# Ordering the down projection of a hybrid decoder block as one list of steps

## The chip, the cores and the metric

The kernel runs on one core of a Trainium2 chip. The metric is the device time of one execution in microseconds (us), lower is better. Three executions of the kernel before are shown; one further execution was profiled.

## What is computed

The reference is one decoder block on 512 tokens of width 2048, in float32. Only its last sub-layer is touched by the change; the rest is named so that the stages can be placed.

```python
mod = silu(c) @ w_ada + b_ada                    # six rows: shift, scale, gate, twice
h = rmsnorm(x, g1) * (1 + sc1) + sh1
mix = concat(rwkv7(h @ w_in), pool(h @ w_in)) @ w_out
x = x + gt1 * mix
h = rmsnorm(x, g2) * (1 + sc2) + sh2
u = h @ w_up                                     # 2048 -> 2 x 5632
val, gate = split(causal_conv3(u) + conv_b)
x = x + gt2 * ((silu(gate) * val) @ w_down)      # 5632 -> 2048: the down projection
out = rmsnorm(x, g_final)
```

## The kernel before

**Precision.** Every float32 product is made of three matmuls (`mm3`, L133): weight and activation are each split into a high part (a cast on ACT) and a low part (a subtraction on DVE), and PE computes high x high (L135), high x low (L136) and low x high (L137). A block of up to eight weight tiles of 128x128 (a 128x1024 row) is split by `wsplit` (L1381): the cast is L1387, the subtraction L1388. The result goes into one of three buffers, `w0`, `w1` and `w2`, in turn, so a cast cannot start before PE has finished with the block three back.

**The down projection** begins after the last pair of the up projection (about 1670 us of 2161). Its 44 activation tiles `ad[j]` lie in device memory. There are 16 output rows of 128 features, and four parts:

- *Plain* (`plain`, L1675): tiles 0 to 7, each of the 16 rows, eight weight tiles with 512 columns: 24 matmuls a row. The result is copied to `yd[f]` in device memory (`stored`, L1697). Between the rows, `operands` prepares the operands of the next part; two of them (T3 and T4) are held back and made later by `last_operands` (L1579).
- *Strassen group* (`strassen`, L1711): tiles 8 to 23, in a 2x2 scheme with seven products per pair of rows instead of eight. For each f from 0 to 7 the order is Y11, (T4 of the f before, in `last_down`, L1703), Y21, T1, T2, Y22, T3; each is 24 matmuls of 256 columns. The weights of T1, T2, Y22 and T3 are sums on DVE over 128x1024 quarters (r1 L1736, r2 L1743, r4 L1750, r3 L1757); r2 needs r1 and r4 needs r2. Partial results are read out by ACT (L1725, L1738, L1745, L1707) and DVE (L1731, L1752, L1759), and added into `yd` by POOL's DMA queue (L1753, L1708).
- *Rest in full width*: tiles 24 to 43 (20 tiles, in blocks of 8, 8 and 4), output rows 0 to 7 with 512 columns. The activations are loaded in place and split (`act_pair_inplace`, L1508: cast L1515, subtraction L1516). The first four rows go through `down_four` (L1816) block by block; the others one after the other.
- *Rest in halves*: the output rows 8 to 15, first for columns 0 to 255, then for 256 to 511 (`down_half`, L1850), in steps of 24, 24 and 12 matmuls.

**Around it.** Each output row needs an element of the last gate `gt2`: `gate_row` (L1807) multiplies a 128x2048 row of `w_ada` with silu(c) on DVE (L1812) and adds the bias (L1813); `gate_load` (L1802) fetches the row two ahead on SP's queue. `load_x2` (L1841) fetches the residual and the `yd` sum and joins them on DVE (L1845). `last_residual` (L1857) adds the row (DVE L1264), squares it (ACT L1255 or L1251), sums the squares (DVE L1256) and scales it (ACT L1859).

**What sets the order.** In this part nothing but the dependences and a priority by the place in the program: a scheduler of the compiler picks each engine's next instruction. Two places say more: the three matmuls of a block that is held back are threaded singly between those of the next block by `tc.issue_after` (in `mm3`), and `gate_row` is queued behind the last weight subtraction in the same way. Other parts of the kernel (L452, L1157) are under `tc.manual_schedule()`, where each engine takes its instructions in the order in which the program emits them. Either way the program of an engine is one fixed list; what differs is who chose its order.

**Buffers.** Weight rows of the plain part and of the rest land in three buffers of `wide` (in the rest two halves of `wd2` besides); the sums r1 to r4 use the same three. The quarters of the Strassen group use two pairs of buffers (`wd4`).

Of the kernel before, what the change touches and what calls it, by code (L numbers as in the profile page):

```python
# [16 lines left out]
P = 128  # L17
# [10 lines left out]
NSLOT = 10  # L28
NB = 10
# [38 lines left out]
def block_kernel(ctx, tc, a, out, stop=None, dbg=None):  # L68
# [64 lines left out]
    def mm3(ps, wh, wl, xh, xl, start, stop, more=False, hold=False):  # L133
# [1374 lines left out]
    def act_pair_inplace(i, u, g, eng):  # L1508
# [70 lines left out]
    def last_operands(name):  # L1579
        for h in held:  # L1580
            if h[0] != name:
                continue
            if len(h) == 4:
                make(name, h[1], pairwise(h[2]), 2, h[3])
                h[2].done()
            else:
                make(*h)
# [87 lines left out]
    def plain(acts, k0):  # L1675

        nk = len(acts)
        for f in range(KT):
            w = wide("wd").rearrange("p a b -> p (a b)")
            nc.sync.dma_start(w, a["wdn"][f, :, k0 * P : (k0 + nk) * P])  # L1680
            wh, wl = wsplit(w, 0)
            ps = bank()
            for k in range(nk):
                sl = slice(k * P, (k + 1) * P)
                mm3(ps, wh[:, sl], wl[:, sl], acts[k][:, 0, :], acts[k][:, 1, :], start=k == 0, stop=k == nk - 1,
                    hold=f == KT - 1 and k == nk - 1)
            if f == 0:
                last_product(pend)
            if f < KT - 1:
                stored(f, ps)  # L1690
            for _ in range(2 if f else 1):
                next(prep, None)
        for _ in prep:
            pass
        return lambda: stored(KT - 1, ps)
# [7 lines left out]
    def last_down(p):  # L1703

        f, u2, b, w22 = p
        product(b, w22, ops["T4"], start=False)
        S.activation(u2[:, H0], b, AF.Copy, scale=-1.0)  # L1707
        G.dma_start(yd[f], u2.t, accum_op=ALU.add)  # L1708
        u2.done()

    def strassen(hook):  # L1711

        wq = [rb.tile([P, 4 * QW], F32, tag=f"x2_{i}", name="wd4") for i in (0, 2, 1, 3)]
        pend = None
        for f in range(NWF):
            wa, wb = wq[2 * (f % 2)], wq[2 * (f % 2) + 1]
            w11, w12, w21, w22 = (t[:, s_] for t in (wa, wb) for s_ in (W1, W2))
            nc.sync.dma_start(wa, a["wdn"][f, :, ND * P : 3 * ND * P])
            nc.sync.dma_start(wb, a["wdn"][f + NWF, :, ND * P : 3 * ND * P])
            pa = bank()[:, 0:HT]  # L1720
            cap = Slot("cap")
            product(pa, w11, ops["Y11"])
            if f == 0:
                finish_plain()
            S.copy(cap[:, H0], pa)  # L1725
            if pend:
                last_down(pend)
            u1 = Slot("u1")
            pb = bank()[:, 0:HT]
            product(pb, w12, ops["Y21"])  # L1730
            V.tensor_add(u1[:, H0], cap[:, H0], pb)  # L1731
            hook(f, 0)
            u2 = Slot("u2")
            pc = bank()[:, 0:HT]
            r1 = wide("r1").rearrange("p a b -> p (a b)")
            V.tensor_add(r1, w21, w22)  # L1736
            product(pc, r1, ops["T1"])
            S.copy(cap[:, H1], pc)  # L1738
            if f == 0:
                last_operands("T3")  # L1740
            hook(f, 1)
            r2 = wide("r2").rearrange("p a b -> p (a b)")
            V.tensor_add(r2, r1, w11)  # L1743
            product(pa, r2, ops["T2"], start=False)
            S.copy(cap[:, H0], pa)  # L1745
            if f == 0:
                last_operands("T4")
            hook(f, 2)
            r4 = wide("r4").rearrange("p a b -> p (a b)")
            V.tensor_add(r4, r2, w12)  # L1750
            product(pc, r4, ops["Y22"], start=False)
            V.tensor_add(u1[:, H1], cap[:, H0], pc)  # L1752
            G.dma_start(yd[f], u1.t, accum_op=ALU.add)  # L1753
            u1.done()
            hook(f, 3)
            r3 = wide("r3").rearrange("p a b -> p (a b)")
            V.tensor_add(r3, w11, w21)  # L1757
            product(pa, r3, ops["T3"], start=False)
            V.scalar_tensor_tensor(u2[:, H1], pa, -1.0, cap[:, H1], op0=ALU.mult, op1=ALU.subtract)  # L1759
            cap.done()  # L1760
            pend = (f + NWF, u2, pa, w22)
        return pend

    def rest_pair(eng):
# [228 lines left out]
```

## Time and profile before

| What | Value |
|---|---|
| median of three runs | 2163.02 us (2159.95 to 2188.56) |
| the profiled execution | 2162.7 us, its span 2160.9 us |
| mean granted TensorE clock | 0.992 |
| PE busy | 2110.9 us, 98% |
| DVE busy | 1678.0 us, 78% |
| ACT busy | 1047.8 us, 48% |
| POOL busy | 237.0 us, 11% |

| Stretch of the trace, us | what runs | PE busy | DVE busy | ACT busy | DMA share |
|---|---|---|---|---|---|
| 1700 to 1750 | plain | 50.00 | 19.56 | 16.78 | 0.47 |
| 1800 to 1850 | Strassen group | 50.00 | 38.28 | 22.66 | 0.55 |
| 1900 to 1950 | its last f, start of the rest | 46.36 | 31.88 | 22.01 | 1.00 |
| 1950 to 2000 | rest, full width | 47.63 | 40.99 | 18.20 | 0.86 |
| 2050 to 2100 | rest, halves | 50.00 | 31.24 | 29.64 | 0.63 |

How to read it. The span is the traced part of an execution; the time of the run is 1.8 us longer. Engine rows give a start, a duration, the engine, the line of the kernel and the tile names, output first; in square brackets stands how long the engine sat idle before and who released it. The ends of matmuls are modelled and matmuls overlap, so their starts are to be compared, not their durations.

### The profile page before, as it was taken

Reading aid. Unit: us, or ns where it says so; the run is one execution under the profiler, and the core shown is the slowest. Engines: PE = TensorE matmul, PEld = TensorE weight load, DVE = VectorE, ACT = ScalarE, POOL = GpSimd, SP = SyncE. Lnnn points to the kernel's source line nnn. Section 1 sums busy time; section 2 is a strip of 40 time slices with the busy share of each in tenths; the row PEclk is TensorE's granted clock in tenths of the full one; section 3 lists DMA queues with packets and bytes.
Section 4 is the critical chain, followed back from the end, with each engine's and each line's share of the span. In section 5 each row is a group of like instructions: output and inputs, shape, how many; then the busy total and the mean of one; then the engine's idle time right before and its main releaser. Section 6 shows DMA issues by size and latency. Waiting matters only on the chain.

```text
span 2160.9 us, 44013 instructions
## 1 busy us (share of the span) xinstructions
PE 2110.9 (98%) x17864; PEld 1866.0 (86%) x17864; DVE 1678.0 (78%) x2615; ACT 1047.8 (48%) x1510; POOL 237.0 (11%) x376
## 2 busy tenths in 40 slices
PE   7999999999999999999999999999999999999997
PEld 3567777777767888999999999999999889987897
DVE  7998898988853678888888887777788657768764
ACT  4354444433433466555555555555556444443353
POOL 0002122221100101110110000000000000120000
PEclk9999999999999999999999999999999999999998
DMA  9976676656537565989888877777777635598764
GB/s 395 393 229 197 200 199 174 199 170 186 150 105 263 183 197 176 290 241 260 253 241 255 236 209 205 207 208 210 209 209 219 211 118 144 161 318 311 243 195 167
DMA packets 169485, 471.89 MB, mean 218 GB/s; under 512 B 21361, under 2 KB 29505, under 8 KB 159169
## 3 DMA queue, kind: packets, MB, share of 16 engines
q1 hardware_dynamic: 120370, 352.12, 48.1%
q0 software_dynamic: 27696, 79.20, 17.5%
q10 hardware_dynamic: 21216, 37.76, 5.7%
q8 instruction: 140, 2.29, 0.4%
q14 instruction: 63, 0.52, 0.1%
HBM read 432.81 MB, written 36.18 MB: 217 GB/s over the span
## 4 chain that ended last, share of the span: by engine, by line
PE 86%; DMA 5%; DVE 4%; ACT 2%; issue 2%; POOL 1%; POOLq 0%; ACTq 0%; DVEq 0%; SPq 0%
PE b L137 19%; PE b L135 19%; PE b L136 19%; PE mm L645 11%; PE pf L426 4%; PE b L1217 2%; PE b L1218 1%; DMA wrow<-wup 1%; PE pb L1047 1%; DVE war L764 1%; DMA wraw<-wout 1%; DMA wa<-ada 1%; PE pa L711 0%; ACT x L1317 0%; DMA wraw<-win 0%
## 5 line engine op out<-in xcount | busy, mean ns | idle before, releaser
L137 PE MATMUL b<-t,uw 128*128 128x256 f32 x1408 | 388.6, 276 | 0.0
L135 PE MATMUL b<-t,uw 128*128 128x256 f32 x1408 | 388.6, 276 | 0.0
L136 PE MATMUL b<-t,uw 128*128 128x256 f32 x1408 | 388.6, 276 | 0.0
L135 PE MATMUL b<-y,uw 128*128 128x256 f32 x1056 | 293.6, 278 | 4.1 <-ACT uw L1387 4.1
L137 PE MATMUL b<-y,uw 128*128 128x256 f32 x1056 | 292.8, 278 | 0.8 <-DVE uw L1388 0.7
L136 PE MATMUL b<-y,uw 128*128 128x256 f32 x1056 | 292.9, 277 | 0.0
L645 PE MATMUL mm<-ahl,whi 128*128 128x512 f32 x864 | 289.7, 409 | 2.1 <-DVE rk L548 1.4
L135 PEld LDWEIGHTS b<-t,uw 128*128 128x128 f32 x1408 | 264.3, 188 | 0.0
L136 PEld LDWEIGHTS b<-t,uw 128*128 128x128 f32 x1408 | 264.3, 188 | 0.0
L137 PEld LDWEIGHTS b<-t,uw 128*128 128x128 f32 x1408 | 264.3, 188 | 0.0
L1388 DVE TENSOR_TENSOR uw<-r,uw 128x1024 fp32r<-128x1024 f32 x164 | 200.6, 1224 | 76.7 <-ACT uw L1387 76.7
L1388 DVE TENSOR_TENSOR uw<-wquart,uw 128x1024 fp32r<-128x1024 f32 x156 | 190.9, 1224 | 68.0 <-ACT uw L1387 67.0
L1387 ACT CAST uw<-wquart 128x1024 fp32r<-128x1024 f32 x156 | 164.1, 1052 | 88.9 <-PE b L137 66.0
L135 PEld LDWEIGHTS b<-y,uw 128*128 128x128 f32 x1056 | 199.5, 189 | 4.8 <-ACT uw L1387 4.8
L137 PE MATMUL b<-act,uw 128*128 128x256 f32 (+1 forms) x608 | 200.5, 330 | 2.7 <-DVE uw L1388 2.7
L1388 DVE TENSOR_TENSOR uw<-wd,uw 128x1024 fp32r<-128x1024 f32 (+1 forms) x112 | 124.1, 1109 | 101.1 <-ACT uw L1387 100.3
L1387 ACT CAST uw<-r 128x1024 fp32r<-128x1024 f32 x164 | 172.5, 1052 | 60.6 <-PE b L137 60.6
L135 PE MATMUL b<-act,uw 128*128 128x256 f32 (+1 forms) x608 | 200.7, 330 | 0.0
L137 PEld LDWEIGHTS b<-y,uw 128*128 128x128 f32 x1056 | 199.5, 189 | 1.2 <-DVE uw L1388 1.2
L136 PE MATMUL b<-act,uw 128*128 128x256 f32 (+1 forms) x608 | 200.4, 330 | 0.0
L136 PEld LDWEIGHTS b<-y,uw 128*128 128x128 f32 x1056 | 199.6, 189 | 0.1
L645 PEld LDWEIGHTS mm<-ahl,whi 128*128 128x128 f32 x864 | 158.2, 188 | 43.2 <-issue 12.2
(356 smaller groups left out, 4601.2 us busy)
## 6 DMA issues: line engine op xcount, KB each, us to landing
wquart<-wup SPq DMA_DIRECT2D x176, 512.0 KB, 5.2
wa<-ada SPq DMA_DIRECT2D x48, 1024.0 KB, 9.1
war<-ada SPq DMA_DIRECT2D x192, 256.0 KB, 3.8
wd<-wdn SPq DMA_DIRECT2D x64, 512.0 KB, 4.1
wraw<-win ACTq DMA_DIRECT2D x118, 256.0 KB, 4.1
wraw<-wout SPq DMA_DIRECT2D x96, 256.0 KB, 3.5
wquart<-wup POOLq DMA_DIRECT2D x44, 512.0 KB, 6.8
r<-wup SPq DMA_DIRECT2D x44, 512.0 KB, 4.7
```

What stands on the lines that cost most here:

```text
L135: muls = [lambda: PE.matmul(ps, wh, xh, start=start, stop=False, skip_group_check=more), lambda: PE.matmul(ps, wh, xl, start=False, stop=F ...
L136: lambda: PE.matmul(ps, wh, xl, start=False, stop=False, skip_group_check=more),
L137: lambda: PE.matmul(ps, wl, xh, start=False, stop=stop, skip_group_check=more)]
L426: PE.matmul(pf[n % 2 * 4 + ii], w[:, sl], full[k], start=k == 0, stop=k == KT - 1)
L645: PE.matmul(ps, w[:, sl], x, start=first, stop=k == KT - 1 and i == 2)
L764: V.scalar_tensor_tensor(wa, wa, 1.0, cqs[kq], op0=ALU.mult, op1=ALU.mult, accum_out=modq[:, kq, j : j + 1])
L1047: PE.matmul(pt[HS[e], h, c * 2 * L : (c + 1) * 2 * L], nt[HS[e], s, :], rw[HS[e], s, :, :], start=True, stop=True)
L1217: PE.matmul(ps[:, :].rearrange("p (a b) -> p a b", a=2), wh, x, start=start, stop=False)
L1218: PE.matmul(ps[:, 0:HT], wl, x[:, 0, :], start=False, stop=stop)
L1387: S.copy(hi, src)
L1388: lo_of[0] = V.tensor_tensor(lo, src, hi.bitcast(F32), op=ALU.subtract)
```

## The change

The whole down projection, with the last product of the up projection as its second entry, becomes a list of `Step` objects. A step has an optional load, a block to split (perhaps after a sum on DVE), its matmuls, and a list of things to do after. `pipeline` emits them: at step i its matmuls, then the load of step i+4, then the sum and split of step i+2, then what follows step i. The matmuls that are held back move their "after" list to the next step. All of this stands under `tc.manual_schedule()`, so each engine and each DMA queue follows this order. `issue_after` goes away in both places.

Other moves: the activations of the rest are loaded (`rest_load`) and split (`rest_split`) at separate steps; T3 is made after the last plain row, T4 after the first two products of the group; loading the residual and joining it are separate (`fetch_x2`, `join_x2`), and the fetches of rows 0 to 3 come in the second block round of the rest, no longer during the group; the gate rows hang on fixed steps. The set of products, sums, splits and transfers is unchanged.

```diff
+LA = 4
...
             for m in (late.pop(0), muls[1], late.pop(0), muls[2], late.pop(0)):
-                with tc.issue_after(ins.ins):
-                    ins = m()
+                ins = m()
...
+    def rest_load(i, eng):
+        u, g = REST[i]
         pool, tag = UNITS[u][g]
         t = pool.tile([P, 2, 2, T], F32R, tag=tag, name="act2")
         for n in range(2):
-            raw = t[:, 1, n, :].bitcast(F32)
-            eng.dma_start(raw, ad[2 * i + n])
-            S.copy(t[:, 0, n, :], raw)
-            V.tensor_tensor(t[:, 1, n, :], raw, t[:, 0, n, :].bitcast(F32), op=ALU.subtract)
-        return [t[:, :, n, :] for n in range(2)]
+            eng.dma_start(t[:, 1, n, :].bitcast(F32), ad[3 * ND + 2 * i + n])
+        A3.extend([t[:, :, n, :] for n in range(2)])
+
+    def rest_split(i):
+        for t in A3[2 * i : 2 * i + 2]:
+            S.copy(t[:, 0, :], t[:, 1, :].bitcast(F32))
+            V.tensor_tensor(t[:, 1, :], t[:, 1, :].bitcast(F32), t[:, 0, :].bitcast(F32), op=ALU.subtract)
...
+    def pipeline(steps):
...
+        def split(st):
+            st.w = wsplit(st.raw(), st.off)
+
+        for i in range(LA):
+            ahead(i, load)
+        ahead(0, split)
+        ahead(1, split)
+        carried = []
+        for i, st in enumerate(steps):
+            st.mm(*st.w)
+            ahead(i + LA, load)
+            ahead(i + 2, split)
+            todo, carried = carried + ([] if st.hold else st.after), st.after if st.hold else []
+            for fn in todo:
+                fn()
...
+    def plain_steps():
...
+            after = [lambda f=f, ps=ps: stored(f, ps[0]), lambda f=f: spread(2 if f > 1 else 1)]
+            if f == KT // 2 + 2:
+                after.append(lambda: pair_load(0))
...
+        out_[-1].after += [lambda: last_operand("T3", 0), lambda: last_operand("T3", 1)]
...
+    def group_steps():
...
+            def total(d, name, x, y):
+                d[name] = wide(name).rearrange("p a b -> p (a b)")
+                V.tensor_add(d[name], x(), y())
+                return d[name]
...
+            out_.append(Step(w11, mul(d, "a", "Y11"), [p1], off=16))
+            if before:
+                out_.append(before)
+            out_ += [Step(w12, mul(d, "b", "Y21"), [p2], off=16),
+                     Step(lambda d=d, x=w21, y=w22: total(d, "r1", x, y), mul(d, "c", "T1"), [p3], off=16),
+                     Step(lambda d=d, y=w11: total(d, "r2", lambda: d["r1"], y), mul(d, "a", "T2", False), [p4], off=16),
+                     Step(lambda d=d, y=w12: total(d, "r4", lambda: d["r2"], y), mul(d, "c", "Y22", False), [p5], off=16),
+                     Step(lambda x=w11, y=w21: total({}, "r3", x, y), mul(d, "a", "T3", False), [p6], off=16)]
+            before = Step(w22, mul(d, "a", "T4", False), [p7], off=16)
             if f == 0:
...
+                out_[0].after.append(lambda: last_operand("T4", 0))
+                out_[1].after += [lambda: last_operand("T4", 1), lambda: pair_load(1)]
+            elif f + 1 < NWF:
+                out_[-5].after.append(lambda f=f: pair_load(f + 1))
+        p = out_[-7:]
+        p[0].after += [lambda: rest_load(0, G), lambda: rest_load(1, G)]
+        p[2].after += [lambda: rest_load(2, G), lambda: rest_load(3, G)]
+        for i in range(4):
+            p[3 + i].after.append(lambda i=i: rest_split(i))
...
     def gate_row():
         i = gated[0]
         gated[0] += 1
-        with tc.issue_after(lo_of[0].ins):
-            m = mod[:, 80 + i : 81 + i]
-            V.scalar_tensor_tensor(wa2[i], wa2[i], 1.0, cb[0], op0=ALU.mult, op1=ALU.mult, accum_out=m)
-            V.tensor_add(m, m, cols("b_ada", 80 + i, 81 + i))
+        m = mod[:, 80 + i : 81 + i]
+        V.scalar_tensor_tensor(wa2[i], wa2[i], 1.0, cb[0], op0=ALU.mult, op1=ALU.mult, accum_out=m)
+        V.tensor_add(m, m, cols("b_ada", 80 + i, 81 + i))
         gate_load(i + 2)
...
+    for b, (k0, n) in enumerate(BLOCKS):
+        for f in range(4):
...
+            if b == 1:
+                st.after.append(lambda f=f: fetch_x2(f))
+            if b == 2:
+                st.after.append(lambda f=f: join_x2(f))
+            if 2 * b + f > 1 and f % 2:
+                st.after.append(gate_row)
+            if b == 2:
+                st.after.append(lambda f=f: residual_of(f, four[f][1]))
+    for f in range(4, NWF):
+        sts, ps = rest_steps(f)
+        sts[0].after += [lambda f=f: fetch_x2(f), gate_row]
+        sts[1].after.append(gate_row)
+        sts[2].after += [lambda f=f: join_x2(f), lambda f=f, ps=ps: residual_of(f, ps)]
+        steps += sts
+    for hf in range(2):
+        for f in range(NWF, KT):
+            sts, ps = rest_steps(f, hf)
+            n = f - NWF
+            if hf == 0:
+                sts[0].after.append(lambda f=f: fetch_x2(f))
+                if n in (0, 2, 4):
+                    sts[1].after.append(gate_row)
+                sts[2].after.append(lambda f=f: join_x2(f))
+            sts[2].after.append(lambda f=f, ps=ps, hf=hf: residual_of(f, ps, hf))
...
+    with tc.manual_schedule():
+        pipeline(steps)
```

More of the change, by code (lines that the diff above doesn't have):

```diff
@@ L1673, in block_kernel, with __init__ @@
     yd = [tc.dram_tile([P, T], F32, name=f"yd{f}") for f in range(KT)]
[L1675 to L1695, printed above, removed]
+    class Step:
+        def __init__(self, raw, mm, after=(), load=None, off=0, hold=False):
+            self.raw, self.mm, self.after, self.load, self.off, self.hold = raw, mm, list(after), load, off, hold
@@ new lines, in pipeline, with ahead, load @@
+    def pipeline(steps):
+        def ahead(i, what):
+            if i < len(steps):
+                what(steps[i])
+        def load(st):
+            if st.load:
+                st.load()
+        def split(st):
[12 more added lines that the diff above has]
+                fn()
@@ L1701, in stored @@
         s_.done()
[L1703 to L1714, printed above, removed]
-        for f in range(NWF):
[L1716 to L1722, printed above, removed]
-            if f == 0:
[L1724 to L1762, printed above, removed]
```

232 lines of the change are left out of this document (145 added, 87 removed).

## The prediction

> **What bounds the kernel now.** I read the whole page first, then the windows of the down projection, then PE's waits in it, then the timeline of single engines around each wait. The page's first line, and four windows in which PE has gaps beside one in which it has none (PE, PEld, DVE, ACT, POOL busy; granted clock; DMA share; GB/s):
>
> ```profile
> span 2160.9 us, 44013 instructions
> ```
> ```profile
> 1900.00:1910.00 10.00, 8.24 (x73) 8.05 (x72) 6.75 (x9) 4.43 (x7) 5.58 (x10) 1.00 0.87 263
> 1910.00:1920.00 10.00, 8.12 (x57) 7.92 (x56) 6.03 (x8) 6.34 (x11) 0.00 (x0) 0.83 1.03 394
> 1970.00:1980.00 10.00, 7.79 (x35) 6.12 (x33) 10.00 (x14) 7.85 (x11) 1.10 (x2) 1.00 0.87 309
> 1980.00:1990.00 10.00, 9.84 (x43) 8.18 (x44) 10.00 (x14) 1.30 (x2) 0.78 (x2) 1.00 0.94 334
> 1800.00:1810.00 10.00, 10.00 (x90) 10.00 (x90) 7.25 (x8) 4.75 (x6) 0.86 (x1) 1.00 0.62 184
> ```
>
> PE is the bound. Its waits from 1660 us to the end, those of the closing norm left out (waiter, releaser: total, times, longest):
>
> ```profile
> PE b L137 <- DVE uw L1388: 4.5, 3, 2.4
> PE b L135 <- ACT cap L1738: 1.9, 1, 1.9
> ```
>
> PE stands still for 4.5 + 1.9 = 6.4 us. The timeline of PE shows the two stops of the last Strassen f, and what follows them:
>
> ```profile
> 1906.01 0.28 PE L136 MATMUL b<-T,uw 128*128 128x256 f32 x1
> 1908.04 0.38 PE L137 MATMUL b<-T,uw 128*128 128x256 f32 x1 [1.75 <-DVE uw L1388]
> ...
> 1910.55 0.28 PE L137 MATMUL b<-T,uw 128*128 128x256 f32 x1
> 1912.70 0.38 PE L135 MATMUL b<-Y,uw 128*128 128x256 f32 x1 [1.88 <-ACT cap L1738]
> ...
> 1914.37 0.42 PE L136 MATMUL b<-Y,uw 128*128 128x256 f32 x1
> ...
> 1917.57 0.31 PE L136 MATMUL b<-T,uw 128*128 128x256 f32 x1
> ```
>
> From 1914.37 to 1917.57 there are 15 starts, 0.213 us apart; at full speed 24 matmuls of this size take 2.72 us (next fence), 0.113 apart. So these two stops were followed by 3.2 us at half rate, in the window with the granted clock of 0.83; cost 15 x 0.10 = 1.5, with its edges 1.6 us. All that an order of work can win here is 6.4 + 1.6 = 8.0 us, 0.37% of the span. The longest stop, 2.4 us, lies at the end of the window from 1970, where DVE is busy for 10.00 of 10 us.
>
> **The change part by part.** It adds and removes no matmul, cast, sum or byte. What it moves is the order on ACT, DVE, POOL and SP. So each term is a lateness: when the split of step i+2 ends against the moment when PE wants it. The rows of a regular period of the group:
>
> ```profile
> 1800.02 1.05 ACT L1387 CAST uw<-wd 128x1024 fp32r<-128x1024 f32 x1 [1.67 <-PE b L137]
> ...
> 1819.06 1.05 ACT L1387 CAST uw<-wd 128x1024 fp32r<-128x1024 f32 x1 [1.67 <-PE b L137]
> ```
> ```profile
> 1801.10 1.23 DVE L1388 TENSOR_TENSOR uw<-wd,uw 128x1024 fp32r<-128x1024 f32 x1 [0.66 <-ACT uw L1387]
> 1804.09 1.23 DVE L1388 TENSOR_TENSOR uw<-r,uw 128x1024 fp32r<-128x1024 f32 x1 [1.77 <-ACT uw L1387]
> 1805.35 1.22 DVE L1757 TENSOR_TENSOR r<-wd,wd 128x1024 f32<-128x1024 f32 x1
> ...
> 1808.07 1.23 DVE L1736 TENSOR_TENSOR r<-wd 128x1024 f32<-128x1024 f32 x1
> 1809.22 0.41 DVE L1731 TENSOR_TENSOR u<-cap,b 128x256 f32<-128x256 f32 x1
> 1809.55 1.22 DVE L1388 TENSOR_TENSOR uw<-r,uw 128x1024 fp32r<-128x1024 f32 x1
> ```
>
> Seven steps take 1819.06 - 1800.02 = 19.04 us, 2.72 a step. Cast to subtraction is 1.08. A 1024-wide DVE operation delays the next by 1.14 (1808.07 to 1809.22) when that stands ready, and by 1.26 (1804.09 to 1805.35) behind one that waited; the 256-wide one by 0.33. In this order r3, and r1 of the next f, are summed well ahead of the casts that read them, between other work. In the list each sum stands directly ahead of its own split on DVE: sum, cast, subtraction, next sum, with no overlap.
>
> *Group, f from 1 to 6.* Zero is the end of T3's matmuls. The cast of w12 starts at 0, its subtraction at 1.08, sum r1 at 2.22, cast 3.47 (sum 1.22 plus 0.03), subtraction 4.55; r2: sum 5.69, subtraction 8.02; u1's addition 9.16; r4: sum 9.49, subtraction 11.82; r3: sum 12.96, subtraction 15.29 to 16.52. PE wants it at 6 x 2.72 = 16.32: 0.2 late. With 1.26 in place of 1.14 it is 0.65. After r3 three steps without sums restore the phase. I take 0.2 x 6 = 1.2 us (long: 0.65 x 6 = 3.9).
>
> *Group, f = 0.* The list puts T3, held over from the last plain row, and half of T4 between r1 and r2, and the rest of T4 between r2 and r4. In the trace r1 of f = 0 was summed in the plain stage, under cover, and the held operands went through back to back, two 512-wide in 1.29, 0.6 each:
>
> ```profile
> 1740.26 1.23 DVE L1736 TENSOR_TENSOR r<-wd 128x1024 f32<-128x1024 f32 x1
> ...
> 1761.90 1.29 DVE L1529 TENSOR_TENSOR T<-t,T 128x512 fp32r<-128x512 f32 x2
> ```
>
> Zero is the start of Y11. PE: Y11 with three held 512-wide matmuls (twice the columns, 0.23 each) ends at 3.4, Y21 at 6.12, T1 at 8.84. The cast of r1 waits for the buffer that the held matmuls read: 1.2; subtraction 2.28; DVE then does T3 (two 512-wide and one 1024-wide, which waits for its cast) and half of T4 until 7.12; sum r2 7.12, subtraction 9.45 to 10.68, wanted at 8.84: 1.85 late. T2 ends at 13.4; T4's second half and sum r4 (12.06) bring r4's subtraction to 15.6: 2.2 late; r3 follows 0.8 late. Sum 4.9 (long: 6.0). Nothing hides it: PE's next block waits.
>
> *Last f.* The four splits of rest activations come after T1, T2, Y22 and T3, each two 512-wide casts and subtractions (1.2 on DVE). Two lie between r4's subtraction and the sum r3: r3's subtraction ends at 17.7 against 16.32, 1.4 late (long 2.7). The stops of 1.75 and 1.88, behind casts that waited for these loads, and the half rate go away: the loads are now ahead of the residual's on POOL.
>
> *Third block round of the rest.* Four steps of 12 matmuls, 2.72 us each, carry four joins, four residuals and two gate rows. The rows for it:
>
> ```profile
> 1956.82 2.28 DVE L1812 SCALAR_TENSOR_TENSOR wa<-wa,cb 128x2048 f32<-128x2048 f32 x1
> ...
> 1959.34 0.75 DVE L1845 SCALAR_TENSOR_TENSOR x<-yd,mod,x 128x512 f32<-128x512 f32 x1
> ...
> 1969.21 0.75 DVE L1264 SCALAR_TENSOR_TENSOR x<-b,mod,x 128x512 f32<-128x512 f32 x1 [1.37 <-PE b L137]
> ```
> ```profile
> 1969.21 0.63 ACT L1387 CAST uw<-wd 128x512 fp32r<-128x512 f32 x1 [2.10 <-PE b L137]
> 1970.00 0.64 ACT L1251 ACTIVATE acc<-x 128x512 f32<-128x512 f32 x1 [0.16 <-DVE x L1264]
> 1970.67 0.82 ACT L1859 ACTIVATE x<-x,eps,vec 128x512 f32<-128x512 f32 x1
> ```
>
> A gate row takes 2.5 (1956.82 to 1959.34). Zero is the start of row 0's block. Residual 0 at 2.72, square 3.5, scaling 4.17, cast of row 3's block 4.9, subtraction 5.55; join 1 6.15; gate row 6.85; residual 1 9.35; square 10.1; scaling 10.8; only then ACT casts the first block of row 4, 11.5 to 12.6, subtraction 12.6 to 13.85. PE wants it at 4 x 2.72 = 10.88: 3.0 late. Behind the gate row of row 3 (19.5 to 22.0) two further blocks are 0.8 and 0.9 late. Sum 4.7 (long 5.8), in place of the stop of 2.4.
>
> *Halves.* Three gate rows hang on the middle step of rows 8, 10 and 12, a row being 2.72 + 2.72 + 1.36 = 6.8 us. DVE needs 1.14 + 1.14 + 0.6 for splits, 0.75 + 0.4 + 0.33 for join, residual and sum, and 2.5: 6.9. The cast of the 12-matmul block stands behind square and scaling, which wait for the residual, which waits for the gate row: some 0.75 late at rows 10 and 12, 1.8 at row 8, where the held row's residual comes on top. Sum 3.3 (long 6.0).
>
> *Elsewhere nothing.* A plain row gives 5.44 us for one split and two operand pieces (1.14 + 2 x 1.14 on DVE); loads four ahead have three buffers, which the split two ahead frees in time. The last column half has no gate row and no join. Taking `issue_after` away leaves PE's order as it was.
>
> *The half rate.* It came after two stops of 1.75 and 1.88 some 4.7 us apart, and not after the single 2.4. At f = 0 stand 1.85 and 2.2 next to one another: I take it once, 1.6 (between 0 and 3.2). [...]
>
> **The sum.** 4.9 + 1.2 + 1.4 + 4.7 + 3.3 + 1.6 = 17.1, less the 8.0 of now: +9.1 us. With the long spacings 6.0 + 3.9 + 2.7 + 5.8 + 6.0 + 3.2 = 27.6, +19.6; short and with no half rate, +7.5. The profiled execution took 2162.7 us (span 2160.9 and 1.8 around it), 0.3 below the median of 2163.02. I forecast 2162.7 + 9.1 = 2171.8 us. I take the short spacings because most of the operations in these places stand ready behind one another.
>
> **The rivals.**
>
> *Not slower.* One mechanism: DVE's lateness stays inside the two steps of lead. It decides at f = 0: if r2's subtraction ends before 8.84, neither it nor r4 stops PE, and if the cast for row 4 is out before 10.88, the third round does not either. Then 8.0 goes and 1.2 + 1.4 comes: 2162.7 - 8.0 + 2.6 = 2157.3 us. For it speaks that the stops of now are all of work set far ahead, in front of near work; against it, that DVE was already full at 1970 to 1980.
>
> *The change does not do what it says.* If the compiler's choice was near the list already, or the list binds only part of the engines, the stops stay where they are: 2160 to 2166 us. Against it speak the sums, made up to half a period earlier now than the list has them.
>
> *Row loads stuck on SP.* `gate_load` waits on SP for its gate row, and the row loads stand behind it. The page's issue group, and the landing times of the row loads (shortest, median, longest):
>
> ```profile
> wa<-ada SPq DMA_DIRECT2D x48, 1024.0 KB, 9.1
> ```
> ```profile
> DMA to landing us min/median/max: 2.6/4.5/13.2
> ```
>
> In the third round the load behind the gate row that ends at 22.0 lands at 26.5 by the median and at 35.2 by the longest; its split, 2.3 us, is wanted at 34.6. So 2.9 us late at worst, and only then; at each of nine gate rows it makes 26 us on top: 2198 us. For it speaks a DMA share of 0.87 and over; against it the median.
>
> **How the numbers follow.** Forecast 0.60 (its own range 2166 to 2182), not slower 0.20, no effect 0.12, stuck loads 0.08. The range reaches to the other cases on both sides: 2157 to 2184 us; below lies half of the second case, above most of the last. Faster by over 2% (43 us, about what a measurement of this kernel can tell from no change) would need five times what is there: 0.01. Slower by over 2%: 0.03, from stuck loads worse than worked out. Within 2%: 0.96.
>
> **What would show it.** Right: in the group, DVE going sum, cast, subtraction without overlap, and a PE stop of some 0.2 to 0.65 us ahead of T3 in each f; stops of about 2 us ahead of T2 and Y22 of f = 0; one of about 3 us ahead of row 4's first block, released by L1388; no stop behind the loads of rest activations. Wrong: PE without stops at f = 0, or ACT waiting for row loads by DMA. The forecast as a whole is wrong if the time is below that of before.

## The result and the profile after

| | before | after |
|---|---|---|
| median of 22 executions each, in turn | 2161.24 us | 2175.58 us |
| median of the 18 shorter executions of each | 2161.19 us | 2174.61 us |
| profiled execution | 2162.7 us | 2173.78 us |
| ratio to before, 95% interval | | 1.0072 (1.0046 to 1.0098) |

Some executions of most kernels here take about 30 us longer than the others; from the second row of the table on the medians leave these out, while the ratios and their intervals still hold a few of them. The change costs 0.72% by the ratio, some 15.6 us, and 13.4 us by the medians of the second row; forecast were 9.1. The page's first line for the kernel after:

```profile
span 2171.9 us, 44015 instructions
```

PE's waits from 1660 us to the end in the kernel after (waiter, releaser: total, times, longest), the closing norm's left out:

```profile
PE b L138 <- DVE uw L1388: 5.8, 13, 0.8
PE b L136 <- ACT uw L1387: 3.4, 3, 1.6
...
PE b L136 <- ACT cap L1812: 1.2, 1, 1.2
```

Before there were 6.4 us in four waits; now there are 10.4 in 17, none longer than 1.6. They stand almost all ahead of a block that has just been split (L1387, L1388). The windows of the kernel after, with the same columns as in the prediction, show where:

```profile
1770.00:1780.00 10.00, 7.79 (x62) 7.17 (x62) 7.64 (x8) 4.53 (x6) 0.01 (x1) 1.00 0.82 316
1800.00:1810.00 10.00, 10.00 (x87) 10.00 (x86) 6.88 (x8) 3.91 (x5) 0.86 (x1) 1.00 0.70 157
1910.00:1920.00 10.00, 9.37 (x77) 8.92 (x77) 7.74 (x10) 7.61 (x13) 0.00 (x0) 1.00 0.56 181
...
2050.00:2060.00 10.00, 7.93 (x60) 7.13 (x60) 4.58 (x6) 4.22 (x6) 1.08 (x2) 1.00 0.96 354
```

The last f of the group (1910) has become nearly whole, f = 0 (1770) and the halves (2050) have got gaps, and in the middle of the group PE is busy for 10.00 of 10 us and yet starts 87 matmuls where it started 90. Busy time does not show that loss; only starts do.

So I measure each part from start to start of PE's matmuls. The first matmul of the plain part, of the group, of the rest in full width and of the halves, and the last one, before:

```profile
1673.88 0.40 PE L135 MATMUL b<-act,uw 128*128 128x512 f32 x1
...
1763.75 0.28 PE L135 MATMUL b<-Y,uw 128*128 128x256 f32 x1
...
1919.89 0.40 PE L135 MATMUL b<-act,uw 128*128 128x512 f32 x1
...
2033.56 0.51 PE L135 MATMUL b<-act,uw 128*128 128x256 f32 x2
...
2144.12 0.28 PE L137 MATMUL b<-act,uw 128*128 128x256 f32 x1
```

and after:

```profile
1668.40 0.40 PE L136 MATMUL b<-act,uw 128*128 128x512 f32 x1
...
1758.04 0.28 PE L136 MATMUL b<-Y,uw 128*128 128x256 f32 x1
...
1919.73 0.40 PE L136 MATMUL b<-act,uw 128*128 128x512 f32 x1
...
2035.08 0.51 PE L136 MATMUL b<-act,uw 128*128 128x256 f32 x2
...
2154.65 0.28 PE L138 MATMUL b<-act,uw 128*128 128x256 f32 x1
```

| us | plain | group | rest, full width | halves | sum |
|---|---|---|---|---|---|
| before | 89.87 | 156.14 | 113.67 | 110.56 | 470.24 |
| after | 89.64 | 161.69 | 115.35 | 119.57 | 486.25 |
| difference | -0.2 | +5.6 | +1.7 | +9.0 | +16.0 |

The down projection takes 16.0 us longer in these two executions, a little more than the ratio and the medians say, though the two spans differ by only 11.0: in the profiled execution of after it began 5.5 us earlier. That start moves between executions; two profiles of one and the same kernel (the seventh and eighth experiments) have it at 1671.21 and 1669.04. The prediction added up terms of the down projection alone, so the parts are the better measure of it. They are one execution each, and two of their terms, the half rate and the spacing of PE's starts, differ between executions of one kernel, as the last experiments show.

### The profile page after: what moved, and what is told of

It is laid out like the page before. It is cut to its first block, busy times and chain, and to the rows that moved or that the text cites. A ratio compares the mean times of both kernels' runs of the same rounds, so it can differ in the third digit from the quotient of the medians.

```text
span 2171.9 us, 44015 instructions
## 1 busy us (share of the span) xinstructions
PE 2122.4 (98%) x17864; PEld 1872.7 (86%) x17864; DVE 1680.3 (77%) x2615; ACT 1044.6 (48%) x1510; POOL 236.4 (11%) x376
## 3 DMA queue, kind: packets, MB, share of 16 engines
q0 software_dynamic: 27696, 79.20, 17.7%
## 4 chain that ended last, share of the span: by engine, by line
PE 81%; issue 6%; DVE 5%; DMA 4%; ACT 3%; POOL 1%; POOLq 0%; ACTq 0%; DVEq 0%; SPq 0%
PE b L138 17%; PE b L137 17%; PE b L136 17%; PE mm L645 10%; PE pf L426 4%; PE b L1217 2%; PE b L1218 1%; PE pb L1047 1%; ACT uw L1387 1%; DVE war L764 1%; ACT x L1317 1%; DMA wa<-ada 1%; PE pa L711 0%; DMA wraw<-win 0%; DVE uw L1388 0%
## 5 line engine op out<-in xcount | busy, mean ns | idle before, releaser
L1388 DVE TENSOR_TENSOR uw<-r,uw 128x1024 fp32r<-128x1024 f32 x164 | 200.5, 1223 | 100.2 <-ACT uw L1387 100.2
L1388 DVE TENSOR_TENSOR uw<-wquart,uw 128x1024 fp32r<-128x1024 f32 x156 | 190.6, 1223 | 68.0 <-ACT uw L1387 67.6
L1387 ACT CAST uw<-r 128x1024 fp32r<-128x1024 f32 x164 | 172.4, 1051 | 108.1 <-PE b L138 55.2
L1387 ACT CAST uw<-wquart 128x1024 fp32r<-128x1024 f32 x156 | 164.0, 1051 | 88.4 <-PE b L138 65.5
L1388 DVE TENSOR_TENSOR uw<-wd,uw 128x1024 fp32r<-128x1024 f32 (+1 forms) x112 | 124.1, 1110 | 70.5 <-ACT uw L1387 70.5
```

What stands on the lines that cost most here:

```text
L1387: S.copy(hi, src)
L1388: lo_of[0] = V.tensor_tensor(lo, src, hi.bitcast(F32), op=ALU.subtract)
```

## The experiments

**What the theory was.** Lateness by order: each engine is bound to the list, DVE takes each sum directly ahead of its own split, and ACT and SP wait in place. Rivals: the moves alone (loads and splits at other places), and the price of the gate rows or of SP's queue by itself. All kernels are the changed kernel with the edit shown. Behind each median stands in brackets that of the kernel before, run beside it; the four numbers behind a ratio are the lengths of the four parts in the profiled execution.

**1. The list without the fixed order.**

```diff
-    with tc.manual_schedule():
-        pipeline(steps)
+    pipeline(steps)
```

> The changed kernel with its list of steps, but without the manual order: the compiler again chooses each engine's next instruction. Theory 'order' (sums directly ahead of their splits, gate rows ahead of residuals, kept so by force, make splits late): most of the loss goes, the stops ahead of T2 and Y22 of f = 0 (4.4 us) and the group's longer period (19.79 for 19.04 us) vanish, 2158 to 2167 us. Rival 'moves' (the places to which the list moves work cost the time, whoever orders it): within 3 us of 2175.6.

Measured: 2165.18 us (before 2159.93), ratio 1.0015 (0.9989 to 1.0040); 90.78, 158.37, 117.10, 110.57 us. The halves are back at the length of before to 0.01 us, f = 0 has no stop, and the group's period is 19.04 again. What is left are a stop in the last f, in PE's timeline of this kernel, and three waits for a weight subtraction, one of them at the start of the plain part and two in the third block round of the rest:

```profile
1911.48 0.58 PE L136 MATMUL b<-Y,uw 128*128 128x256 f32 x1 [5.36 <-ACT cap L1812]
```
```profile
PE b L138 <- DVE uw L1388: 5.1, 3, 2.6
```

Behind the last f's stop and behind the longest of the three PE also went at half rate (granted clock 0.67 from 1910 to 1920 and 0.83 from 1980 to 1990). It follows that most of the loss comes with the fixed order: 486.25 - 476.82 = 9.4 of the 16.0 us by the parts, all of the halves' 9.0 among them; by the ratios 0.57 of 0.72%. That the moves by themselves are free is not shown: 6.6 us by the parts and 5.3 by the medians remain over before, though the interval of the ratio holds 1.

**2. Sums one step earlier.** The sum of a step is emitted with step i + 3, its split stays at i + 2, for r1 to r4.

```diff
+        def add(st):
+            if st.early:
+                st.r = st.raw()
...
-            st.w = wsplit(st.raw(), st.off)
+            st.w = wsplit(st.raw() if st.r is None else st.r, st.off)
...
+            ahead(i + 3, add)
             ahead(i + 2, split)
```

> The changed kernel with the sums r1, r2, r4 and r3 emitted three steps ahead, not directly ahead of their splits; all else as in the list. Theory 'order': the three late splits of f = 0 (4.4 us) fall below 0.5 us, and the group's period goes from 19.79 back to 19.04 us, 5.3 us over seven f; in all 9 to 10 us less, 2165 to 2167 us. Rival 'rate' (PE's 0.118 us between matmuls in the group, for 0.113 before, is a state of PE that no late split causes): only the stops go, the spacing in the group stays at 0.118, 2171 us.

Measured: 2166.34 us (before 2159.93), ratio 1.0046 (1.0005 to 1.0087); 89.44, 151.96, 116.12, 118.03 us. The group lost 9.7 us against after and is 4.2 shorter than before; two stops of 0.5 and 0.9 us stay at f = 0, where the theory had under 0.5. DVE in one f of the group, first in the kernel after (a sum, its subtraction, and the subtraction of r3), then with the early sums (the sums are L1797 there):

```profile
1802.35 1.22 DVE L1791 TENSOR_TENSOR r<-wd 128x1024 f32<-128x1024 f32 x1
1804.74 1.23 DVE L1388 TENSOR_TENSOR uw<-r,uw 128x1024 fp32r<-128x1024 f32 x1 [1.17 <-ACT uw L1387]
...
1815.69 1.23 DVE L1388 TENSOR_TENSOR uw<-r,uw 128x1024 fp32r<-128x1024 f32 x1 [1.17 <-ACT uw L1387]
```
```profile
1802.09 1.22 DVE L1797 TENSOR_TENSOR r<-r,wd 128x1024 f32<-128x1024 f32 x1
1803.55 1.23 DVE L1388 TENSOR_TENSOR uw<-r,uw 128x1024 fp32r<-128x1024 f32 x1 [0.25 <-ACT uw L1387]
```

In the kernel after DVE stands idle for 1.17 us between a sum and its subtraction, the time in which ACT casts that very sum. With one step more the next sum fills most of it: here 0.25 us are left. The rival is not ruled out by this run. Experiment 9 ran the same list in the group at 0.118 us a matmul and took 157.36 there; at that spacing the early sums win 4.3 of the 9.7 us, and the other 5.4 are the spacing of this execution.

**3. Short gate rows.** Gate rows from the fourth on multiply 16 of their 2048 columns on DVE; their loads stay whole.

```diff
-        V.scalar_tensor_tensor(wa2[i], wa2[i], 1.0, cb[0], op0=ALU.mult, op1=ALU.mult, accum_out=m)
+        c_ = slice(0, D if i < 3 else 16)
+        V.scalar_tensor_tensor(wa2[i][:, c_], wa2[i][:, c_], 1.0, cb[0][:, c_], op0=ALU.mult, op1=ALU.mult, accum_out=m)
```

> The changed kernel with the gate rows from the fourth on cut to 16 of their 2048 columns (0.1 us for 2.3 us on DVE; the dot products are left out to that extent, loads and order stay). Theory 'order': the stops in the third round (2.5 us and 1.6 us of half rate) and those in the halves (about 6 us) go: 2164 to 2168 us. Rival 'loads' (row loads stand behind gate loads on SP): the loads stay, so the stops stay, within 3 us of 2175.6.

Measured: 2166.02 us (before 2159.93), ratio 1.0061 (1.0027 to 1.0095); 89.24, 162.31, 111.63, 114.71 us. The median is where the theory has it. The rest in full width wins 3.7, the halves 4.9. So 4.9 of the halves' 9.0 are the 2.3 us of a gate row on DVE; 4.1 remain with rows of 16 columns, where the theory had no stop left. ACT still waits 17.7 us in all for row loads from 1960 to 2160 us (16.5 in the kernel after), so part of the rival stands too.

**4. The residual one step later.** The residual of each row of the rest but the eighth (DVE L1264, square and scaling on ACT) is emitted behind the matmuls of the step that follows it in the list.

```diff
+    for i, st in enumerate(steps):
+        if id(st) in late_of:
+            nxt = steps[i + 1] if i + 1 < len(steps) else st
+            nxt.after[:0] = late_of[id(st)]
```

> The changed kernel with the residual of each row of the rest done one step later, behind the split of the step after, so that no cast stands behind a residual's square and scaling on ACT. Theory 'order': the stops of the third round fall from 2.5 to below 1 us, the half rate goes with them, and the halves lose 2 to 4 of their 6 us: 2167 to 2171 us. Rival 'full' (DVE simply has more work there than PE, in any order): within 1.5 us of 2175.6.

Measured: 2173.60 us (before 2159.93), ratio 1.0072 (1.0038 to 1.0107); 90.34, 162.39, 111.25, 120.96 us. The third block round lost its stop and its half rate (115.35 to 111.25, 4.1 us). The halves did not win the 2 to 4 us expected but gave back 1.4, about what a stretch at half rate costs (1.6 in the third block round of the kernel after), and this profile has one there (granted clock 0.83 from 2050 to 2060). Neither forecast time was met; the gain that remains, some 1 us, is too small to be shown. Among ACT's waits from 1960 to 2160 us is one group for row loads, in the kernel after and in this one:

```profile
ACT uw L1387 <- DMA wd<-wdn: 16.5, 14, 3.3
```
```profile
ACT uw L1387 <- DMA wd<-wdn: 33.4, 16, 3.8
```

Before, ACT waited for no row load in this stretch. With the later residuals the wait doubles. SP's timeline of the kernel after, beside DVE's, shows why a load comes late:

```profile
2033.33 1.68 SPq L1734 DMA_DIRECT2D wd<-wdn  x3
2045.07 0.33 SPq L1882 DMA_DIRECT2D wa<-ada  x1
2045.49 4.82 SPq L1734 DMA_DIRECT2D wd<-wdn  x5
```
```profile
2042.75 2.28 DVE L1888 SCALAR_TENSOR_TENSOR wa<-wa,cb 128x2048 f32<-128x2048 f32 x1
```

SP issues nothing from 2035.01 to 2045.07: the gate load L1882 is next and waits until DVE has read the gate row that lies in its buffer (2042.75 + 2.28 = 2045.03). The five row loads behind it leave only then, and the cast at 2051.59 waits for the first of them, in ACT's timeline:

```profile
2051.59 1.04 ACT L1387 CAST uw<-wd 128x1024 fp32r<-128x1024 f32 x1 [2.37 <-DMA wd<-wdn]
```

**5. Gate loads and the first half's stores on POOL's queue.**

```diff
-            nc.sync.dma_start(wa2[i], a["ada3"][i, :, :])
+            G.dma_start(wa2[i], a["ada3"][i, :, :])
...
-                sts[0].after.append(lambda n=n: finish(H0, n - 3, norm["rstd"]))
+                sts[0].after.append(lambda n=n: finish(H0, n - 3, norm["rstd"], V, G))
```

> After, with two kinds of transfers issued by POOL and not by SP: the loads of the gate rows (L1882) and the four stores of the first half's outputs (L1918). SP is left with the row loads. Theory (the row loads stand on SP behind gate loads that wait for DVE): ACT's waits for the row loads in 1960 to 2160 us (after: 16.5 us in 14 waits, before: none) fall to under 3 us, and of the 7 to 8 us of stops of PE in the halves those ahead of a cast that waited for its load go, some 4 us; the third block round keeps its stop of 2.5 us and the group its 4.4 us and its slower spacing. Time 2171 (2168 to 2173), 3 to 5 us under after. Rival (the gate row itself on DVE, 2.2 us ahead of the sub, makes the stops, and the load only came late because nothing pressed it): the waits go but the stops stay, time as after, 2174 to 2176.

Measured: 2170.59 us (before 2161.13), ratio 1.0015 (0.9977 to 1.0053); 89.24, 162.50, 115.36, 116.50 us. The halves win 3.1, and ACT's wait for row loads from 1960 to 2160 us is all but gone:

```profile
ACT uw L1387 <- DMA wd<-wdn: 1.7, 1, 1.7
```

The theory holds, and the rival with no effect of the queue falls.

**6. The edits of 2 and 5 together:** early sums, and SP for the row loads.

> The two edits that each took one cause away, together: the sums emitted one step earlier, and the gate loads and the first half's stores on POOL. Theory (the causes are separate and add): the early sums gave 7 to 8 us against after (2168.0), the queue gives its 3 to 5 as in the run with it alone: 2164 (2161 to 2166), ratio to before 1.002 (1.000 to 1.004); PE's stops from 1960 to 2160 us down to some 5 us. Rival (the early sums already gave DVE enough slack in the halves, so that the queue no longer matters): 2167 to 2168 as with the sums alone. Nothing forecasts under 2159.

Measured: 2161.60 us (before 2161.13), ratio 0.9956 (0.9915 to 0.9998); 89.24, 151.96, 115.38, 115.66 us. The group is that of experiment 2, the halves are 2.4 shorter than there: two causes, and they add. The four parts sum to 472.24, 2.0 more than before, and the medians are level, where the ratio puts it 0.44% below; that this version beats before is not shown.

**7 and 8. The edits of 2, 4 and 5 together, and the same kernel once more.**

> The last kernel and, with it, the residual of each row of the rest one step later, which on top of after took 4 us of stops and half rate out of the third block round and gave them back in the halves, where ACT's casts waited 33.4 us in all for row loads that stood on SP. Theory (it was given back through SP's queue): with the gate loads off SP the gain of the third block round stays and the halves lose no more than in the last kernel: 2161 (2158 to 2164). Rival (the later residual holds the squares on ACT and so the casts themselves): ACT's waits for loads are gone, the stops past 2110 us stay, and the time is 2165 to 2168.

Measured: 2157.04 us (before 2161.13), ratio 0.9981 (0.9948 to 1.0014); 89.24, 151.96, 111.10, 116.04 us. With the row loads behind the gate loads on SP the later residual won next to nothing; with the gate loads gone from there, the 4.3 us of the third block round stay (115.38 to 111.10) and the halves lose only 0.4. PE's waits from 1660 us to the end in this kernel, without the closing norm, are one row:

```profile
PE b L138 <- DVE uw L1388: 3.5, 7, 0.7
```

> The kernel with all three edits (sums one step earlier, gate loads and first half's stores on POOL, residuals of the rest rows one step later) once more, with runs of the kernel before beside it, since its interval against before (0.9948 to 1.0014) still holds 1. Theory (its lead over before is the 8 us of before's own stops less some 5 us of its own, 3 us or more): 2158 (2156 to 2161), ratio 0.998 (0.996 to 1.000). Rival (no lead, the first run was lucky): 2160 to 2163, ratio 0.999 to 1.001.

Measured: 2155.97 us (before 2159.23), ratio 0.9985 (0.9975 to 0.9995); 89.24, 151.96, 111.10, 115.40 us. This version is faster than before, by 3.2 us, and by 2.5 us by the parts (467.70 against 470.24). What it still loses against before are 5 us in the halves.

**9. The edits of 2 and 4,** with the queue as in the change.

> The early sums and the later residuals, with the gate loads and the first half's stores still on SP. Theory (what the later residual wins in the third block round is given back through SP's queue): ACT waits 20 us or more in all for row loads between 1960 and 2160 us, the stops past 2110 us that the later residual alone brought are there, and the time is that of the early sums alone, 2168 (2165 to 2171). Rival (the two edits on the order are enough, the queue was a side show): 2158 to 2162, as with all three.

Measured: 2166.12 us (before 2159.23), ratio 1.0034 (1.0018 to 1.0049); 89.24, 157.36, 111.20, 122.77 us. Against experiment 2 the rest in full width wins 4.9 and the halves lose 4.7, with ACT waiting 40.9 us for row loads:

```profile
ACT uw L1387 <- DMA wd<-wdn: 40.9, 17, 5.0
```

That is the theory, and the time is that of experiment 2. The group took 157.36, though its list is that of experiment 2 (151.96): see the last two.

**10. DVE's order alone set free.** All engines but DVE keep the list.

```diff
-    with tc.manual_schedule():
+    with tc.manual_schedule(engines={mybir.EngineType.PE, mybir.EngineType.Activation, mybir.EngineType.Pool, mybir.EngineType.SP}):
```

> After, with every engine but DVE kept in the emitted order; DVE's order is left to the builder, as in before. Theory (DVE's order, the sum of a step behind the sub of the step before, is what costs): the stops at f=0 and the slower spacing of the group go, and so does the third block round's stop, some 12 us: 2164 (2161 to 2168), as with the order left free on all engines (2165.2). Rival (the order of ACT or SP costs as much: casts behind squares that wait for DVE, row loads behind gate loads): the group is mended and the halves keep 5 us or more of stops and ACT's waits for row loads: 2168 to 2171.

Measured: 2169.76 us (before 2161.13), ratio 1.0029 (0.9976 to 1.0081); 89.24, 151.33, 119.53, 119.53 us. Half of each: the group is mended, as the theory has it, but the rest in full width got worse than after by 4.2, with stops like this one in PE's timeline:

```profile
1969.10 0.79 PE L138 MATMUL b<-act,uw 128*128 128x512 f32 x1 [2.52 <-DVE uw L1388]
```

Fixing four engines and leaving the fifth free is no middle way in this kernel. The halves stayed at 119.53, but not for the reason of the kernel after: ACT waits for no row load from 1960 to 2160 us here, against the rival, whose time was met. DVE took a gate row, for whose load it had waited 6.0 us, ahead of a subtraction that PE wanted; one stop of 3.0 us followed, and behind it PE went at half rate for most of 10 us (the window has the columns of the prediction; the granted clock is 0.52):

```profile
2040.00:2050.00 10.00, 8.34 (x35) 7.76 (x36) 6.49 (x10) 4.86 (x7) 0.00 (x0) 0.52 0.51 138
```

**11 and 12. Two kernels once more, for PE's spacing.** After a stop of 0.51 us at 1766.24 the group of experiment 9 ran at 0.118 us a matmul, where the same list had run at 0.113 in experiments 2, 6, 7 and 8.

> The kernel with early sums and later residuals once more, for one profile. In its first profile PE's matmuls of the group stood 0.118 us apart from a stop of 0.51 us at 1766 us on, though no split of the group was late after f = 0; the other kernels with the same list in the group (early sums) stood at 0.113. Theory (the spacing is drawn anew by an interruption of PE's stream, whatever the kernel): with two interruptions at f = 0 it is more likely 0.113 this time, and the group takes 152 us in place of 157.4. Rival (the place of this kernel's work or transfers fixes it): 0.118 from the same stop on, 157.4 us.

Measured: 2164.30 us, one execution; 89.24, 151.95, 112.20, 124.00 us. The same kernel, the same stop at f = 0, and this time 0.113 through the group: the spacing belongs to the execution, not to the kernel. The rival falls.

> The changed kernel itself once more, for one profile. Theory (each late split of T3 stops PE while the spacing is 0.113, and each such stop draws the spacing anew; at 0.118 the late split is covered and nothing draws again): the group ends at 0.118 again, perhaps after some f with a stop of 0.5 us ahead of T3 at 0.113, and takes 161 to 163 us. Rival (the spacing is luck of the execution alone): 0.113 through the whole group, with a stop of some 0.5 us in every f. The half rate after the stop of the third block round: by the theory of chance it may be there, at f = 0, or nowhere.

Measured: 2176.95 us, one execution; 89.24, 161.75, 115.36, 120.39 us. Half rate stood at f = 0 and once in the halves (granted clock 0.87 from 1770 to 1780, 0.86 from 2050 to 2060). PE ran at 0.113 from f = 1 to the sixth period, with a stop ahead of T3 in each, and at 0.118 after the last of these rows:

```profile
1800.12 0.28 PE L137 MATMUL b<-T,uw 128*128 128x256 f32 x1
1800.74 0.38 PE L138 MATMUL b<-T,uw 128*128 128x256 f32 x1 [0.34 <-DVE uw L1388]
...
1820.40 0.38 PE L138 MATMUL b<-T,uw 128*128 128x256 f32 x1 [0.34 <-DVE uw L1388]
...
1899.06 0.38 PE L138 MATMUL b<-T,uw 128*128 128x256 f32 x1 [0.34 <-DVE uw L1388]
```

From 1800.12 to 1800.74 it is 0.62 instead of 0.11, a stop of 0.5; with the matmul behind it each f loses 0.62 (period 1820.40 - 1800.74 = 19.66 against 19.04).

## Why the prediction was right or wrong

The direction was right and most of its reason too: DVE's lateness under the list, with nothing to hide it. What the sum did not hold are row loads late on SP and a second spacing of PE's starts. The size was 9.1 us and came out at 16.0 by the parts, 13.4 by the medians. Step by step:

- **Group, f = 0: right.** The stops in the kernel after:

```profile
1767.63 0.39 PE L136 MATMUL b<-T,uw 128*128 128x256 f32 x1 [0.57 <-ACT uw L1387]
1768.89 0.39 PE L138 MATMUL b<-T,uw 128*128 128x256 f32 x1 [0.75 <-DVE uw L1388]
...
1772.92 0.38 PE L136 MATMUL b<-Y,uw 128*128 128x256 f32 x1 [1.24 <-ACT cap L1812]
1773.91 0.39 PE L138 MATMUL b<-Y,uw 128*128 128x256 f32 x1 [0.49 <-DVE uw L1388]
...
1777.44 0.38 PE L138 MATMUL b<-T,uw 128*128 128x256 f32 x1 [0.48 <-DVE uw L1388]
```

  A stop costs the distance from the start before it, less 0.113, so some 0.16 more than the wait in the bracket: 1.65 ahead of T2, 2.07 ahead of Y22, 0.65 ahead of T3, 4.4 us. Predicted were 1.85, 2.2 and 0.8. Ahead of Y22 the last to come was T1's read-out (L1812), which stands behind the cast of r4 in ACT's list; the prediction had only the split there.
- **Group, f from 1 on: mis-sized, 1.2 for 5.3 us.** I took 0.2 for each f, with 0.65 as the long value, and named a stop ahead of T3 in each f as the sign. The repeat of the kernel has that stop, at 0.62 for each f. The first profile has no stop at all from 1778 to 1915 us; about the same time is lost there in PE's spacing, which was not in the prediction, as ACT's cast of w12 in one f and the next shows:

```profile
1800.12 1.05 ACT L1387 CAST uw<-wd 128x1024 fp32r<-128x1024 f32 x1 [1.73 <-PE b L138]
1803.66 1.05 ACT L1387 CAST uw<-r 128x1024 fp32r<-128x1024 f32 x1 [0.34 <-DVE r L1791]
...
1819.91 1.05 ACT L1387 CAST uw<-wd 128x1024 fp32r<-128x1024 f32 x1 [1.73 <-PE b L138]
```

  The period is 19.79 against 19.04, 0.75 in each of seven (f = 7, the last f, has the same spacing up to its stops). What was too short in the repeat, and would have been here at 0.113, is the link from sum to cast: I had 1.25 from the sum's start to the cast's; the rows have 1803.66 - 1802.35 = 1.31 (the sum's row stands in experiment 2), and there are four links. So r3's subtraction ends 1815.69 + 1.23 - 1800.12 = 16.8 us after the cast of w12 starts, not 16.52; that is 0.5 late at a spacing of 0.113, and just in time at 0.118, which wants it at 6 x 24 x 0.1178 = 16.96.
- **Last f: right.** 1.0 us in place of 1.4; the stops of 1.75 and 1.88 and their half rate are gone.
- **Half rate: one, as predicted, but not at f = 0 in this execution.** It came in the third block round; in the other four profiles with the change's own sums in fixed order (experiments 3, 4, 5 and 12) it came at f = 0, with starts 0.21 apart up to 1778.41, 1780.57, 1781.24 and 1780.69 us, and in experiments 4 and 12 once more in the halves. The rows of the third block round:

```profile
1978.78 0.50 PE L136 MATMUL b<-act,uw 128*128 128x512 f32 x1 [1.61 <-ACT uw L1387]
...
1980.50 0.63 PE L136 MATMUL b<-act,uw 128*128 128x512 f32 x1
1980.93 0.63 PE L137 MATMUL b<-act,uw 128*128 128x512 f32 x1
...
1983.49 0.46 PE L137 MATMUL b<-act,uw 128*128 128x512 f32 x1
```

  Starts 0.43 apart instead of 0.23 for 3.0 us cost 1.6. In the repeat of the kernel, where PE meets the same stops (1.60 and 0.53 in the brackets), the third block round had none: the granted clock is 1.00 from 1970 to 1990.
- **Third block round: right in place, too large in this profile.** It lost some 4.2 us (115.35 less the 111.10 of experiment 7, which has no stop there), but 1.6 of these are the half rate, which the prediction had as a term of its own: 2.5 of stops for 4.7. The first stop was 2.5, not 3.0, and the further 0.8 and 0.9 did not come. In the repeat they came, as 0.4 and 0.7 in the timeline around 1994 and 1998, without the half rate, and there the 4.7 stand against 4.3.
- **Halves: mis-sized, 3.3 for 9.0; this is the step that failed.** My term held three gate rows on DVE. The short rows show 4.9 for them. The other part I had set apart as the rival "row loads stuck on SP", at 2.9 us late for each of nine gate rows, or not at all. It was there, but small: 3.1 us by experiment 5. It belonged into the sum. ACT waiting for row loads by DMA was also the sign that I had named for being wrong, and it came: 16.5 us in 14 waits. About 1 us remains. Experiment 5's 3.1 are net of some 1.2 us by which PE's wider spacing lengthened the halves of that profile (932 starts outside the stops, 0.1152 apart on the mean, 0.1139 in the kernel after), so the spacing alone is of the size of what remains. A kernel with short gate rows and gate loads off SP together was not run; that these two add is not shown.
- **Elsewhere nothing: right.** The plain part is 0.2 shorter.
- **Rivals.** "Not slower" fell with its own deciding point, r2's subtraction at f = 0, which came late. "The change does not do what it says" fell with DVE's rows: sum, cast, subtraction, next sum, as in the list.

The sum with the measured terms: 4.4 + 5.3 + 1.0 + 4.2 + 9.0 = 23.9, less before's 8.0, is +15.9, against +16.0 by the parts. That the forecast missed by 6.9 us of the parts and not by more is in part luck: the group from f = 1 on and the halves were too small by 9.8, the third block round with the half rate too large by 2.1, f = 0 and the last f by 0.9.

## What to carry to other kernels

A list that fixes every engine's order needs a lead for each link of a chain, not one for the whole: with sum and split at the same step, DVE idled 1.17 us for each cast, and one step more for the sums won 9.7 us in the group of one profile and 4.3 in that of another, 8.3 us of the whole time by the medians. A load that waits for a consumer does not belong on the queue of loads that must run ahead: off it, ACT's waits for row loads fell from 16.5 to 1.7 us. Look in the waits for a DMA queue released by a compute engine, and price it by what stands behind it. And moving work later only pays where the next engine's lead holds: the same edit was worth 1 us or less with the gate loads on SP, and some 4 us without them.

## What was not expected of the hardware

**Two spacings of the same matmul.** 256-wide matmuls start 0.1133 or 0.1178 us apart, at a granted clock of 1.00 in both cases (from 1770 to 1900 us before, from 1780 to 1910 after) and for 140 us at a time. Here are the first matmuls of Y22 and of T3, 24 starts apart, in the kernel after and then in experiment 12 at the same stage (2.83 and 2.72 us):

```profile
1794.27 0.28 PE L136 MATMUL b<-Y,uw 128*128 128x256 f32 x1
...
1797.10 0.28 PE L136 MATMUL b<-T,uw 128*128 128x256 f32 x1
```
```profile
1797.29 0.28 PE L136 MATMUL b<-Y,uw 128*128 128x256 f32 x1
...
1800.01 0.28 PE L136 MATMUL b<-T,uw 128*128 128x256 f32 x1
```

In the group of these profiles it changed only where PE's stream was interrupted or its clock changed: in the kernel after at the stop ahead of T3 at 1777.44, in experiment 5 the starts are 0.21 apart up to 1781.24 and 0.118 behind. It ended at 0.118 in all five profiles with the change's own sums in fixed order (the two of the change, and experiments 3, 4 and 5), and in one of six with early sums. That fits a draw at each stop, with the slow spacing covering the late split so that no further stop follows; it is argued, not shown. In the halves it is no draw at one place: before, after and in experiments 4, 11 and 12 the starts are 0.118 apart from the closing norm's four small matmuls (L184) to its next two (L197), and 0.113 behind those, though PE waits for nothing there. Before, 58 starts lie between the last two rows, 0.1178 apart:

```profile
2095.47 0.50 PE L184 MATMUL b<-cmat,acc 128*128 128x1 f32 x4
...
2096.03 0.28 PE L136 MATMUL b<-act,uw 128*128 128x256 f32 x1
...
2102.86 0.28 PE L137 MATMUL b<-act,uw 128*128 128x256 f32 x1
```

In all five it is 0.118 between the same rows and 0.113 behind them; what sets it stays open.

**The half rate did not go by the length of a stop alone.** Before, two stops of 1.75 and 1.88 us were followed by it (granted clock 0.83 from 1910 to 1920 us) and the single one of 2.4 was not (1.00 from 1970 to 1990). The stop of the third block round (1.77 and 0.7 us) was followed by it in the change's first profile (0.83 from 1980 to 1990) and in experiment 6 (0.83 from 1970 to 1980), and not in the repeat (1.00 from 1970 to 1990). In the first profile the stretch at half rate is 3.0 us by the starts and 3.4 by the granted clock (1.7 of 10 us missing, at half rate). What decides whether a stop is followed by it is not shown by any run here.
